# A hybrid decoder layer on one core: the u projection by channel, and a buffer for each row of x

## The chip, the core and the metric

The kernel runs on one core of a Trainium2 chip. TensorE (PE in the rows) multiplies, VectorE (DVE), ScalarE (ACT) and GpSimd (POOL) work on what it leaves, and SyncE (SP) issues nearly all transfers. The metric is the time of the device in microseconds for one execution of the program, taken as the median of several runs. Where a profile is read, it is that of one execution, and its time stands beside the median below.

## The reference

One layer of a decoder on 1024 prompt tokens and 8 sample tokens (1032 columns in all), 1024 channels. Only the first part matters here: a norm, one projection whose columns are split, and a state-space branch that eats the part called u.

```python
h = rms_norm(x, norm1_g)
proj = h @ w_in                        # 1024 x (512 q | 128 k | 128 v | 512 u | 2048 gates)
u = proj[..., o3:o4]                   # 512 channels = 32 groups of 16
...
attn_out = attend(q, k, v, sinks)      # window of 128
ug = u.reshape(B, T, 32, 16)
bu = einsum('gph,btgh->btgp', bb, ug)  # each group drives a complex state of 64
h  = associative_scan(...)             # over positions
y  = einsum('ghp,btgp->btgh', c, h) + d * u
z  = gelu(y); ssm_out = z * sigmoid(z @ w_glu + b_glu)
merged = sigmoid(g_a) * (attn_out @ w_a) + sigmoid(g_s) * (ssm_out @ w_s)
x = x + merged @ w_out;  x = x + swiglu_ffn(rms_norm(x)); y = rms_norm(x)
```

For the sample tokens the attention reads a window of 128 old keys and values (`state_k_win`, `state_v_win`), and the window moved on by one token is an output.

## The kernel before

All of it is f32. A product is done as three products of f32r halves (high x high, high x low, low x high), so each operand is split in two: `XH[k]`, `XL[k]` are the halves of row k of x (128 channels x 1032 tokens, k = 0 to 7), already multiplied by the norm's gain; `wuh`, `wul` are those of the u weights.

**The opening stage** (lines 178 to 274). For each row k, SP loads `xr` (three buffers of one tag, line 204), GpSimd issues the load of `wr` (line 211), ACT makes `XH` (L216), the squares `sq` (L224) and `wuh` (L214), DVE makes `XL` (L217), `wul` (L219) and adds the squares (L225). PE then multiplies by token: `umm(ps, k, slice(s, TP, 8))` holds every eighth column of x as the stationary operand (128 tokens of residue s modulo 8) and streams the 512 u channels, for s = 0 to 6 row by row as the rows come. After the last row, `rc` sums the squares over the channels (L232), `rstd` makes `rcol`, `uevac` takes each bank with the token's scale into `ut[b]`, then residue 7 and the eight sample tokens (`us`, with 8 stationary columns) follow, transposes turn the sample part, and `across` spreads `rcol` into `r1`, a row of scales by token.

**After it** come the projections k, v and four q (`load_w`, `mm3`, lines 467 to 512; three f32r matmuls of 344 columns for each of 8 rows and 3 chunks, 72 for a block of 128 channels). `load_w` passes weights through `wraw` (3 buffers), `wh` and `wl` (3 each): a load waits until the one three before it has been split. v is turned by transposes `vtp` (L490) that need `vt`, which DVE makes (L484). The attention's tables `msk`, `snk` and `snks` are loaded by SP; DVE makes `nsnk` from `snk` (L442). Then attention, its projection, the state-space stage (`group4`, eight times), and the feed-forward.

**In `group4`** four transposes (L805) turn `ut` into `ug`, ACT copies it to `UG` (L808), and both `sps` (L814) and `y` (L871) use `UG`.

**The order** on each engine is set by a scheduler at build time (`tc.block(schedule_with_timeline_sim=True)`), not by the text; each engine then runs its list in order and waits where an operand isn't there. The built program also makes each transfer of SP wait until the one some eight places ahead of it in the list has landed. Tags name places in memory: `Zl0` to `Zl3`, `Zh2`, `Zh3` and `s2` are of 128 x 1032 f32 and are used one after the other by what the text puts there.

## Time and profile before

| | |
|---|---|
| median of 3 runs | 1440.84 us (1439.7 to 1446.9) |
| the profiled execution | 1441.37 us, its span 1439.6 us |
| PE busy | 1362.9 us, 95% of the span |
| DVE, ACT, POOL busy | 874.7 (61%), 567.4 (39%), 460.4 us (32%) |
| PE clock by slices of 36 us | 0.9 or more of full speed, but 0.7 in the second, 0.8 in two later ones, 0.6 in the last |
| moved by DMA | 136.59 MB, 95 GB/s on the mean |

PE is the bound nearly everywhere: of the 40 slices of the page, PE shows 9 tenths or more in most. Two slices cover the opening stage. The rows below are read as follows: a timeline row gives when an instruction (or a run of like ones, x7) started, how long it was busy, its line, what it wrote from what, and in brackets how long its engine had been idle and what ended that.

### The profile page before, as it was taken

The numbers are of one execution on the slowest core, as the hardware profiler recorded it, in microseconds if no ns is written. First come the engines' busy times: TensorE is split into PE (matmuls) and PEld (weight loads), VectorE is DVE, ScalarE is ACT, GpSimd is POOL, SyncE is SP. The second block draws the span as 40 slices with busy tenths as digits, with TensorE's granted clock in tenths as the row PEclk, the third lists the DMA queues.
The fourth block names the chain that finished last, engine by engine and source line by source line (L and its number), as shares of the span: only waits on it lengthen the run. The fifth ranks groups of instructions, "written<-read, shape, count | busy, mean of one in ns | idle before, by whom it ended". The sixth has DMA issues, their size and how long they took to land. (4 is left out here: it accounts for less than half of the span.)

```text
span 1439.6 us, 25893 instructions
## 1 busy us (share of the span) xinstructions
PE 1362.9 (95%) x10031; PEld 1324.8 (92%) x10031; DVE 874.7 (61%) x1792; ACT 567.4 (39%) x1121; POOL 460.4 (32%) x411
## 2 busy tenths in 40 slices
PE   7699999998899999998899999999999999999995
PEld 6689999997788999997899999999999999999995
DVE  4575986259999744736485444444344674775864
ACT  3323656423344622434353333333333442433551
POOL 1113321156674000125144333333332132232352
PEclk9799999999989999999899999999999999999996
DMA  6102000121111201253534332332223882542413
GB/s 221 62 19 79 16 24 22 37 66 40 40 30 36 66 30 45 81 177 118 175 110 126 114 118 99 101 104 82 93 95 119 270 272 60 163 140 65 132 34 118
DMA packets 84731, 136.59 MB, mean 95 GB/s; under 512 B 15737, under 2 KB 27521, under 8 KB 84608
## 3 DMA queue, kind: packets, MB, share of 16 engines
q1 hardware_dynamic: 83248, 131.61, 28.8%
q0 software_dynamic: 640, 2.10, 0.5%
q8 instruction: 79, 1.29, 0.4%
q10 hardware_dynamic: 720, 1.23, 0.2%
q14 instruction: 44, 0.36, 0.1%
HBM read 103.59 MB, written 30.12 MB: 93 GB/s over the span
## 5 line engine op out<-in xcount | busy, mean ns | idle before, releaser
L126 PE MATMUL wo<-mh,wl_wo 128*128 128x258 f32 x256 | 74.0, 290 | 4.9 <-DVE wl_wo L114 4.9
L124 PE MATMUL wo<-mh,wh_wo 128*128 128x258 f32 x256 | 74.4, 290 | 2.5 <-ACT wh_wo L113 1.8
L125 PE MATMUL wo<-ml,wh_wo 128*128 128x258 f32 x256 | 73.7, 288 | 0.0
L126 PE MATMUL gs<-xh,wl_gs 128*128 128x344 f32 x192 | 61.7, 322 | 0.0
L124 PE MATMUL gs<-xh,wh_gs 128*128 128x344 f32 x192 | 61.6, 322 | 0.0
L125 PE MATMUL gs<-xl,wh_gs 128*128 128x344 f32 x192 | 61.5, 321 | 0.0
L1066 POOL TENSOR_TENSOR ws_d<-wr_1d,ws_d 128x512 f32<-128x512 f32 (+1 forms) x13 | 17.5, 1347 | 117.8 <-issue 74.5
L126 PEld LDWEIGHTS wo<-mh,wl_wo 128*128 128x128 f32 x256 | 49.9, 195 | 5.3 <-DVE wl_wo L114 5.3
L124 PEld LDWEIGHTS wo<-mh,wh_wo 128*128 128x128 f32 x256 | 50.1, 196 | 3.2 <-ACT wh_wo L113 3.2
L125 PEld LDWEIGHTS wo<-ml,wh_wo 128*128 128x128 f32 x256 | 49.9, 195 | 0.0
L126 PE MATMUL ga<-xh,wl_ga 128*128 128x344 f32 x144 | 47.5, 330 | 1.5 <-DVE wl_ga L114 1.5
L1066 POOL TENSOR_TENSOR ws_u<-wr_1u,ws_u 128x512 f32<-128x512 f32 x9 | 11.6, 1285 | 116.4 <-issue 116.4
L124 PE MATMUL ga<-xh,wh_ga 128*128 128x344 f32 x144 | 48.3, 335 | 0.0
L125 PE MATMUL ga<-xl,wh_ga 128*128 128x344 f32 x144 | 48.0, 333 | 0.0
L114 DVE TENSOR_TENSOR wl_wo<-wr_wo,wh_wo 128x512 fp32r<-128x512 f32 x32 | 23.0, 719 | 38.8 <-ACT wh_wo L113 38.7
L199 PE MATMUL u<-wuh,xh 128*128 128x512 f32 x64 | 24.8, 470 | 18.9 <-ACT wuh L214 17.1
L465 POOL TENSOR_TENSOR ml<-mg,mh 128x344 fp32r<-128x344 f32 x6 | 6.6, 1140 | 106.3 <-ACT mh L464 106.3
L199 PEld LDWEIGHTS u<-wuh,xh 128*128 128x128 f32 x64 | 19.2, 331 | 20.7 <-ACT wuh L214 17.4
L547 ACT ACTIVATE P<-P,st 128x256 f32<-128x256 f32 (+1 forms) x64 | 31.0, 486 | 17.5 <-DVE st L544 17.5
L113 ACT CAST wh_wo<-wr_wo 128x512 fp32r<-128x512 f32 x32 | 19.8, 620 | 41.4 <-PE wo L125 39.1
L124 PEld LDWEIGHTS gs<-xh,wh_gs 128*128 128x128 f32 x192 | 36.1, 188 | 0.0
L126 PEld LDWEIGHTS gs<-xh,wl_gs 128*128 128x128 f32 x192 | 36.0, 188 | 0.0
(2596 smaller groups left out, 5875.5 us busy)
## 6 DMA issues: line engine op xcount, KB each, us to landing
hr<-hid SPq DMA_DIRECT2D x77, 258.0 KB, 3.6
wr_wo<-in_wout SPq DMA_DIRECT2D x32, 256.0 KB, 2.9
wr_0g<-in_wfg SPq DMA_DIRECT2D x17, 256.0 KB, 3.1
wr_1g<-in_wfg SPq DMA_DIRECT2D x17, 256.0 KB, 2.9
wr_0u<-in_wfu SPq DMA_DIRECT2D x17, 256.0 KB, 2.7
wr_1u<-in_wfu SPq DMA_DIRECT2D x17, 256.0 KB, 2.6
xres<-in_xT SPq DMA_DIRECT2D x16, 258.0 KB, 3.8
x1d<-mg SPq DMA_DIRECT2D x16, 258.0 KB, 2.8
```

Source lines behind the costliest of these rows:

```text
L113: S.copy(wh[:, 0:w], raw[:, 0:w])
L114: (eng or V).tensor_tensor(wl[:, 0:w], raw[:, 0:w], f32(wh[:, 0:w]), op=ALU.subtract)
L124: TE.matmul(ps, wh, xh[:, cs], start=(k == 0), stop=False)
L125: TE.matmul(ps, wh, xl[:, cs], start=False, stop=False)
L126: TE.matmul(ps, wl, xh[:, cs], start=False, stop=(k == n - 1))
L199: TE.matmul(ps, XH[k][:, cs], wuh[:, k], start=(k == 0), stop=False)
L465: eng.tensor_tensor(lo, src, f32(hi), op=ALU.subtract)
L547: S.activation(Pt[:, i, 0:W], Pt[:, i, 0:W], AF.Exp, bias=nm_[:, i:i + 1], scale=0.125, accum_out=ds[:, i:i + 1])
L1066: P.tensor_tensor(t, x, y, op=op)
```

## The change

Four things are changed, and what depends on them.

1. **u by channel.** The u weights are now the stationary operand (128 channels m = 0 to 3) and x streams, in three chunks of 344 tokens: `umm(ps, m, k, c)`. The sample tokens ride in the last chunk. m = 0 and 1 take six banks and run row by row as the rows of x come; m = 2 and m = 3 run after the last row. The scale by token is now a product with `r1`, which lies along the columns, in `uput`; m = 1 is first taken unscaled by ACT and multiplied in place later.
2. **Reordered through DRAM.** `uput` writes `SG[m]` (channel, t, c) for token 8c + t, with the t steps 128 elements apart. `ushift` stores `SG[m]` to DRAM (`ud`) and loads it again in eight pieces of 16 partitions as `UGA[m]`, in the layout in which `group4` wants it. So the transposes `ug` and the copies `UG` are gone from `group4`, which takes a view of `UGA`.
3. **A buffer for each row of x.** The eight `xr` now lie in `Zl0` to `Zl3`, `Zh2`, `Zh3`, `s2` and one of their own; `ident` is loaded after the last row, and `wur` has five buffers where it had three.
4. **`Vs` whole.** The old values are loaded as 128 partitions where 127 were loaded; the host rolls the window, so that the last partition holds what is overwritten later.

```diff
@@ -174,14 +174,13 @@
     XM = [(XH[k], XL[k]) for k in range(KD)]
     r1 = main.tile([128, T], F32, tag="r", name="r1")
 
-
-    ut = [main.tile([128, 8, 8, 16], F32, tag=f"Zl{b}", name=f"ut{b}") for b in range(4)]
-
     ssmp = tc.tile_pool(name="ssmp", bufs=1, side="left")
     sp = ssmp.__enter__()
     usT = sp.tile([128, 4, NS], F32, tag="usT", name="usT")
 
 
+    ud = ctx.enter_context(tc.tile_pool(name="ud", bufs=1, space=bass.MemoryType.DRAM))
+    UGA = [None] * 4
     with tc.tile_pool(name="p1", bufs=1, side="left") as p1, \
             tc.tile_pool(name="p1r", bufs=1, side="right") as p1r:
         ssum = p1r.tile([128, T], F32, tag="ssum", name="ssum")
@@ -193,23 +192,26 @@
         wps = aux("warm", "pv")
         for i in range(12):
             TE.matmul(wps, warm[:, 0:128], warm, start=True, stop=True)
-        ups = [acc(f"u{s}") if s < 3 else aux(f"u{s}") for s in range(7)]
-
-        def umm(ps, k, cs):
-            TE.matmul(ps, XH[k][:, cs], wuh[:, k], start=(k == 0), stop=False)
-            TE.matmul(ps, XH[k][:, cs], wul[:, k], start=False, stop=False)
-            TE.matmul(ps, XL[k][:, cs], wuh[:, k], start=False, stop=(k == KD - 1))
-
+
+        def umm(ps, m, k, c):
+            wh, wl = wuh[:, k, 128 * m:128 * m + 128], wul[:, k, 128 * m:128 * m + 128]
+            TE.matmul(ps[:, :CH], wh, XH[k][:, chunk(c)], start=(k == 0), stop=False)
+            TE.matmul(ps[:, :CH], wh, XL[k][:, chunk(c)], start=False, stop=False)
+            TE.matmul(ps[:, :CH], wl, XH[k][:, chunk(c)], start=False, stop=(k == KD - 1))
+
+        UP = {(0, c): acc(f"u0{c}") for c in range(NCH)}
+        UP.update({(1, c): aux(f"u1{c}", "xxy"[c]) for c in range(NCH)})
         for k in range(KD):
-            xr = p1r.tile([128, T], F32, tag="xr", name=f"xr{k}", bufs=3)
-            wr = p1r.tile([128, 512], F32, tag="wur", name=f"wur{k}", bufs=3)
+            tag = ("Zl0", "Zl1", "Zl2", "Zl3", "Zh2", "Zh3", "s2", "xr")[k]
+            xr = (main if k < KD - 1 else p1r).tile([128, T], F32, tag=tag, name=f"xr{k}")
+            wr = p1r.tile([128, 512], F32, tag="wur", name=f"wur{k}", bufs=5)
             if k == 0:
                 for c in range(NCH):
                     (S if c == 1 else SY).dma_start(xr[:, chunk(c)], h["xT"][k][:, chunk(c)])
             else:
                 SY.dma_start(xr, h["xT"][k])
             P.dma_start(wr, h["wu"][k])
-            if k == 1:
+            if k == KD - 1:
                 SY.dma_start(ident, h["ident"])
             S.copy(wuh[:, k], wr)
             for cs in ([chunk(c) for c in range(NCH)] if k == 0 else [slice(0, T)]):
@@ -223,55 +225,79 @@
                 sq = p1r.tile([128, T], F32, tag="sq", name=f"sq{k}", bufs=1)
                 S.activation(sq, xr, AF.Square)
                 V.tensor_tensor(ssum, ssum, sq, op=ALU.add)
-            if k == KD - 1:
-
-                rc = aux("rc", "pv")
-                rcs = p1r.tile([128, 18], F32, tag="rcs", name="rcs")
-                V.memset(rcs, 1.0)
+            for m in range(2):
+                for c in range(NCH):
+                    umm(UP[m, c], m, k, c)
+
+
+        SG = [None] * 4
+        C8 = CH // 8
+
+        def uput(m, c, r):
+            if SG[m] is None:
+                SG[m] = main.tile([128, 8, 128], F32, tag=f"Zl{m}", name=f"sg{m}")
+            w = CH if c < NCH - 1 else CH - NS
+            dst = SG[m][:, :, c * C8:c * C8 + w // 8].rearrange("p t c -> p c t")
+            src = UP[m, c][:, 0:w].rearrange("p (c t) -> p c t", t=8)
+            if r:
+                V.tensor_tensor(dst, src, r1[:, c * CH:c * CH + w].rearrange("p (c t) -> p c t", t=8), op=ALU.mult)
+            else:
+                S.copy(dst, src)
+            if w < CH:
+                if r:
+                    V.tensor_tensor(usT[:, m], UP[m, c][:, w:CH], r1[:, TP:T], op=ALU.mult)
+                else:
+                    S.copy(usT[:, m], UP[m, c][:, w:CH])
+
+        def ushift(m):
+
+            t = ud.tile([128, 8, 128], F32, tag=f"ud{m}", name=f"ud{m}")
+            SY.dma_start(t, SG[m])
+            UGA[m] = main.tile([128, 8, 128], F32, tag=f"Zl{m}", name=f"ug{m}")
+            for i in range(8):
+                SY.dma_start(UGA[m][16 * (7 - i):16 * (8 - i)], t[:, i].rearrange("(g h) c -> h g c", h=16))
+
+        for c in range(NCH):
+            uput(1, c, False)
+
+        rc = aux("rc", "pv")
+        rcs = p1r.tile([128, 18], F32, tag="rcs", name="rcs")
+        V.memset(rcs, 1.0)
+        for c in range(NCH):
+            UP[2, c] = aux(f"u2{c}", "yxx"[c])
+            for k in range(KD):
+                umm(UP[2, c], 2, k, c)
+            if c == 0:
                 for s in range(8):
-                    TE.matmul(rc[:, 2 * s:2 * s + 2], ssum[:, s:TP:8], ones[:, 0:2], start=True, stop=True)
+                    colsum(rc, 2 * s, [ssum], 128 * s, 128)
                 colsum(rc, 16, [ssum], TP, NS)
                 V.tensor_copy(rcs[:, 0:16], rc[:, 0:16])
                 V.tensor_copy(rcs[:NS, 16:18], rc[:NS, 16:18])
                 rcol = rstd(p1r.tile([128, 4, 18], F32, tag="rcol", name="rcol"), rcs, 18)
-            for s in range(7):
-                umm(ups[s], k, slice(s, TP, 8))
-
-        def uevac(s, ps):
-            for b in range(4):
-                dst = ut[b][:, :, 7 - s, :]
-                src = ps[:, b * 128:(b + 1) * 128].rearrange("p (g h) -> p g h", h=16)
-                if s % 2 == 0:
-                    S.activation(dst, src, AF.Copy, scale=rcol[:, 2 * s:2 * s + 1])
-                else:
-                    V.tensor_scalar(dst, src, rcol[:, 2 * s:2 * s + 1], None, op0=ALU.mult)
-
-        for s in range(7):
-            uevac(s, ups[s])
-        u7 = aux("u7")
-        for k in range(KD):
-            umm(u7, k, slice(7, TP, 8))
-        uevac(7, u7)
-        usp = acc("us")
-        for k in range(KD):
-            umm(usp[:NS], k, slice(TP, T))
-        usm = p1r.tile([NS, 512], F32, tag="usm", name="usm")
-        V.tensor_scalar(usm, usp[:NS], rcol[:NS, 16:17], None, op0=ALU.mult)
-        ust = aux("ust", "pv")
-        for b in range(4):
-            TE.transpose(ust[:, b * NS:(b + 1) * NS], usm[:, b * 128:(b + 1) * 128], ident[:NS, :NS])
-        V.tensor_copy(usT, ust[:, 0:4 * NS].rearrange("p (b t) -> p b t", b=4))
-
-        r1v = r1[:, 0:TP].rearrange("p (c t) -> p t c", t=8)
         for q in range(3):
-            rp = aux(f"r1p{q}")
+            rp = aux(f"r1p{q}", ("pv", "y", "pv")[q])
             if q < 2:
                 for i in range(4):
                     across(rp, 128 * i, rcol[:, 8 * q + 2 * i:8 * q + 2 * i + 1], 128)
-                S.copy(r1v[:, 4 * q:4 * q + 4], rp.rearrange("p (t c) -> p t c", t=4))
+                S.copy(r1[:, 512 * q:512 * q + 512], rp)
             else:
                 across(rp, 0, rcol[:, 16:17], NS)
                 S.copy(r1[:, TP:T], rp[:, 0:NS])
+        for c in range(NCH):
+            uput(0, c, True)
+        ushift(0)
+        V.tensor_tensor(SG[1], SG[1], r1[:, 0:TP].rearrange("p (c t) -> p t c", t=8), op=ALU.mult)
+        V.tensor_tensor(usT[:, 1], usT[:, 1], r1[:, TP:T], op=ALU.mult)
+        ushift(1)
+        for c in range(NCH):
+            uput(2, c, True)
+        ushift(2)
+        for c in range(NCH):
+            UP[3, c] = acc(f"u3{c}")
+            for k in range(KD):
+                umm(UP[3, c], 3, k, c)
+            uput(3, c, True)
+        ushift(3)
 
         def pt(name, shape=(128, 48), pool=None):
             return (pool or sp).tile(list(shape), F32, tag=name, name=name)
@@ -442,7 +468,7 @@
     V.tensor_scalar(nsnk, snk, -1.0, None, op0=ALU.mult)
     SY.dma_start(snks, h["sinks_s"])
     SY.dma_start(Ks, h["ks"])
-    SY.dma_start(Vs[0:127], h["vs"])
+    SY.dma_start(Vs, h["vs"])
     for c in range(NCH):
         V.tensor_tensor(Cr[:, chunk(c)], Cr[:, chunk(c)], r1[:, chunk(c)], op=ALU.mult)
         V.tensor_tensor(Sr[:, chunk(c)], Sr[:, chunk(c)], r1[:, chunk(c)], op=ALU.mult)
@@ -799,13 +825,7 @@
         for s in range(8):
             SY.dma_start(M[16 * s:16 * s + 16, :, 16 * (7 - s):128], kt[:, :, 0:16 * (s + 1)])
 
-
-        tp = aux(f"ug{hb}", "x")
-        for i in range(4):
-            TE.transpose(tp[:, i * 128:(i + 1) * 128],
-                         ut[b][:, 4 * half + i].rearrange("p a b -> p (a b)"), ident)
-        UG = t4("UG", (128, 4, 128), 2)
-        S.copy(UG.rearrange("p a b -> p (a b)"), tp)
+        UG = UGA[b][:, 4 * half:4 * half + 4]
 
 
         next(fill, None)
...
-    a["vs"] = vs[:, 1:].transpose(1, 0, 2)
+    a["vs"] = np.roll(vs, -1, axis=1).transpose(1, 0, 2)
```

What the scheduler makes of it is shown at three places.

SP at the start of the program, before: `xr3` to `xr6` are the fourth to seventh rows of x, `Cr` and `Sr` the rotary tables, `Ks` and `Vs` the old keys and values, `wr_k`, `wr_v` the weights of k and v.

```order
L437 DMA Cr_761<-in_rope_c 128x1032
L438 DMA Sr_762<-in_rope_s 128x1032
L444 DMA Ks_763<-in_ks 128x1024
L210 DMA xr3_224<-in_xT 128x1032
L445 DMA Vs_764<-in_vs 127x1024
L107 DMA wr_k_0_784<-in_wst 128x512
L107 DMA wr_k_512_790<-in_wst 128x512
L107 DMA wr_v_0_904<-in_wst 128x512
L210 DMA xr4_256<-in_xT 128x1032
L210 DMA xr5_288<-in_xT 128x1032
L210 DMA xr6_320<-in_xT 128x1032
L107 DMA wr_v_512_910<-in_wst 128x512
```

And after (the first six rows of x stand ahead of these, with no other load between them):

```order
L212 DMA xr6_298<-in_xT 128x1032
L212 DMA xr7_327<-in_xT 128x1032
L215 DMA ident_66<-in_ident 128x128
L315 DMA sgn_618<-in_sgn 128x1
L320 DMA prm_624<-in_prm 128x144
L463 DMA Cr_860<-in_rope_c 128x1032
L464 DMA Sr_861<-in_rope_s 128x1032
L107 DMA wr_k_0_883<-in_wst 128x512
L107 DMA wr_k_512_889<-in_wst 128x512
L107 DMA wr_v_0_1003<-in_wst 128x512
L470 DMA Ks_862<-in_ks 128x1024
L471 DMA Vs_863<-in_vs 128x1024
```

All eight rows of x are now issued ahead of every other load of SP; before, three of them stood behind `Vs` and three weight loads, and the last behind three more.

SP later, after: `ud1`, `ud2`, `ud3` are the stores of u to DRAM and `ug0` to `ug3` the loads that bring it back (eight each), `snk` the sinks from which DVE makes `nsnk`.

```order
L258 DMA ug1_493<-ud1_491 16x8x128 x8
L258 DMA ug2_509<-ud2_507 16x8x128 x8
L255 DMA ud3_598<-sg3_543 128x1024
L258 DMA ug3_600<-ud3_598 16x8x128 x8
L107 DMA wr_q1_0_1233<-in_wst 128x512
L107 DMA wr_q1_512_1239<-in_wst 128x512
L501 DMA out_kwp<-ro_k2_995 128x128
L503 DMA out_kws<-Ks_862 128x1024
L465 DMA msk_865<-in_mask 128x256
L466 DMA snk_866<-in_sinks 128x8
```

The same stretch before has no transfer of u in it:

```order
L107 DMA wr_q0_0_1016<-in_wst 128x512
L107 DMA wr_q0_512_1022<-in_wst 128x512
L210 DMA xr7_352<-in_xT 128x1032
L439 DMA msk_766<-in_mask 128x256
L440 DMA snk_767<-in_sinks 128x8
L443 DMA snks_768<-in_sinks_s 64x1
L107 DMA wr_q1_0_1134<-in_wst 128x512
L107 DMA wr_q1_512_1140<-in_wst 128x512
L475 DMA out_kwp<-ro_k2_896 128x128
L477 DMA out_kws<-Ks_763 128x1024
```

Thirty-six transfers of u now stand between the first weights of q0 and those of q1, and `msk`, `snk` and `snks`, which stood ahead of q1's weights, now stand behind them and behind two outputs.

DVE around `nsnk`, before (`kl` is the low half of k, `vt` is v with its scale):

```order
L465 TENSOR_TENSOR kl_758<-ro_k0_826,kh_757 128x344
L460 TENSOR_TENSOR ro_k1_861<-ro_k1_861,rs_k1_858 128x344
L442 TENSOR_SCALAR nsnk_773<-snk_767 128x8
L465 TENSOR_TENSOR kl_758<-ro_k1_861,kh_757 128x344
L456 STREAM_SHUFFLE rs_k2_893<-rr_k2_891 128x344
L459 TENSOR_TENSOR ro_k2_896<-k2_866,Cr_761 128x344
L460 TENSOR_TENSOR ro_k2_896<-ro_k2_896,rs_k2_893 128x344
L476 COPY Ks_763<-ro_k2_896 128x8
L465 TENSOR_TENSOR kl_758<-ro_k2_896,kh_757 128x344
L484 TENSOR_TENSOR vt_916<-v0_917,r1_83 128x344
L484 TENSOR_TENSOR vt_916<-v1_943,r1_83 128x344
L484 TENSOR_TENSOR vt_916<-v2_969,r1_83 128x344
```

and after:

```order
L510 TENSOR_TENSOR vt_1015<-v0_1016,r1_83 128x344
L491 TENSOR_TENSOR kl_857<-ro_k0_925,kh_856 128x344
L491 TENSOR_TENSOR kl_857<-ro_k1_960,kh_856 128x344
L491 TENSOR_TENSOR kl_857<-ro_k2_995,kh_856 128x344
L468 TENSOR_SCALAR nsnk_872<-snk_866 128x8
L510 TENSOR_TENSOR vt_1015<-v1_1042,r1_83 128x344
L510 TENSOR_TENSOR vt_1015<-v2_1068,r1_83 128x344
L519 TENSOR_TENSOR vl_859<-vtp0_1095,vh_858 128x512
L524 COPY vsm_1111<-vts_1109 8x128
```

`nsnk`, which waits for `snk`, stood ahead of the last `ro_k` and of all three `vt`; now it stands between the first `vt` and the other two, and PE's transposes `vtp` stand right behind the last product of v on PE in both.

## Rows read from the trace of the kernel before

**Rows 1.** Who waited for whom: total us, times, longest; 0 to 130 us.

```profile
PE u L199 <- ACT wuh L214: 17.1, 1, 17.1
```

**Rows 2.** Stretches: busy us (count) of PE, PEld, DVE, ACT, POOL; clock, DMA share, GB/s.

```profile
10.00:20.00 10.00, 10.00 (x38) 9.45 (x38) 9.13 (x25) 7.41 (x9) 1.61 (x3) 0.89 0.79 302
38.00:40.00 2.00, 0.00 (x0) 0.00 (x0) 0.00 (x0) 0.00 (x0) 0.00 (x0) 0.50 0.07 27
30.00:48.00 18.00, 0.87 (x3) 0.55 (x2) 2.07 (x4) 5.11 (x7) 3.71 (x3) 0.57 0.41 137
70.00:77.00 7.00, 7.00 (x20) 5.64 (x21) 5.64 (x32) 3.43 (x13) 0.00 (x0) 0.51 0.00 0
296.00:460.00 164.00, 145.15 (x937) 135.04 (x936) 146.03 (x287) 61.99 (x130) 112.11 (x120) 0.95 0.15 41
```

**Rows 3.** Timeline (start us, us, engine, line, operation) of SP's issues, 0 to 140.

```profile
9.95 0.56 SPq L445 DMA_DIRECT2D Vs<-in_vs  x1
10.80 15.81 SPq L107 DMA_DIRECT2D wr_k<-in_wst  x2
28.19 6.37 SPq L210 DMA_DIRECT2D xr<-in_xT  x3
```

**Rows 4.** Timeline of PE in the opening stage and in the k projection.

```profile
7.85 2.87 PE L199 MATMUL u<-wuh,xh 128*128 128x512 f32 x7 [1.79 <-ACT xh L216]
...
47.42 3.38 PE L199 MATMUL u<-wuh,xh 128*128 128x512 f32 x7 [17.13 <-ACT wuh L214]
...
67.16 3.74 PE L232 MATMUL rc<-ones,ssum 128*128 128x2 f32 x16
...
90.89 0.40 PE L124 MATMUL k<-xh,wh_k 128*128 128x344 f32 x1
...
94.47 0.32 PE L125 MATMUL k<-xl,wh_k 128*128 128x344 f32 x1
...
96.05 0.32 PE L126 MATMUL k<-xh,wl_k 128*128 128x344 f32 x1
```

**Rows 5.** Weight loads grouped by line (busy us, mean ns), 60 to 90 and 90 to 112.

```profile
L199 PEld LDWEIGHTS u<-wuh,xh 128*128 128x128 f32 x22 | 7.3, 331 | 0.3
...
L124 PEld LDWEIGHTS k<-xh,wh_k 128*128 128x128 f32 x24 | 4.5, 188 | 0.0
```

**Rows 6.** Timeline of ACT and DVE over one row of x.

```profile
9.51 1.16 ACT L216 ACTIVATE xh<-xr,vec 128x1032 fp32r<-128x1032 f32 x1 [0.76 <-DMA xr<-in_xT]
...
10.70 1.29 DVE L217 SCALAR_TENSOR_TENSOR xl<-xr,vec,xh 128x1032 fp32r<-128x1032 f32 x1 [2.29 <-ACT xh L216]
...
12.04 1.16 ACT L216 ACTIVATE xh<-xr,vec 128x1032 fp32r<-128x1032 f32 x1
...
13.66 0.18 DVE L310 TENSOR_SCALAR t<-prm 128x48 f32<-128x48 f32 x1
```

**Rows 7.** PSUM copies, ns min/median/max, and one DVE product from PSUM (timeline).

```profile
L271 ACT COPY r<-r1p x2: 1159/1194/1228, 90.7 to 91.7; 128x512 f32<-128x512 f32 x2
L808 ACT COPY UG<-ug x8: 566/567/584, 323.4 to 453.8; 128x512 f32<-128x512 f32 x8
...
105.50 0.50 DVE L459 TENSOR_TENSOR ro_k<-k,Cr 128x344 f32<-128x344 f32 x1
```

**Rows 8.** Small pieces on SP and their landing: timeline; issues with KB, us to landing.

```profile
100.76 0.43 SPq L440 DMA_DIRECT2D snk<-in_sinks  x1
...
324.16 5.20 SPq L800 DMA_DIRECT2D M<-kt  x8
...
bc<-in_bc SPq DMA_DIRECT2D x4, 256.0 KB, 3.1
```

**Rows 9.** Timeline of DVE at `nsnk` and at the last chunk of v.

```profile
104.31 0.17 DVE L442 TENSOR_SCALAR nsnk<-snk 128x8 f32<-128x8 f32 x1 [0.68 <-DMA snk<-in_sinks]
...
114.32 0.52 DVE L484 TENSOR_TENSOR vt<-v,r 128x344 f32<-128x344 f32 x1 [3.25 <-PE v L126]
```

**Rows 10.** Timeline of PE: the four transposes of one `group4`.

```profile
320.58 0.60 PE L805 MATMUL ug<-ident,ut 128*128 128x128 f32 x4
```

## The prediction

> **What bounds the kernel now.** I read the stretches first, then the waits, then the timeline of SP and PE in the first 115 us. PE is the bound almost everywhere, so a change pays for the PE time that it removes, and for holes in PE, and for nothing else unless it opens a hole. There is one large hole in the stage that the change touches: between 30 and 48 us PE was busy for 0.87 us of 18, at a clock of 0.57 on the mean, and DMA, too, at 0.41 of its share [rows 2]. The wait behind it is the longest of PE in the stage, 17.1 us for `wuh` [rows 1]; ACT makes `wuh` behind `xh`, which waits for a row of x. SP shows why the row was late: `Vs` was issued at 9.95, the two weight loads behind it held SP for 15.81 us, and the next three rows of x went out only at 28.19 [rows 3]. In the middle of the hole DMA moved 27 GB/s at a share of 0.07, which is one engine of 16 [rows 2]: something was passing through a single engine while all else had to wait. `Vs`, of 127 partitions, is the only load here of that odd shape. PE began u at 7.85, went on at 47.42 after 17.13 us of nothing, and reached the first product of k at 90.89 [rows 4]. So the stage up to k takes 90.9 us.
>
> **What the change does to the stage.** I build the time of k's first product anew.
>
> *Rows of x.* All eight are issued ahead of all else, into buffers of their own. Rows and u weights are 6.3 MB; at the 302 GB/s of 10 to 20 us [rows 2] the last lands at about 23, earlier if the rate is higher. The engines that split them are slower than that: ACT needs 12.04 - 9.51 = 2.53 us a row, DVE 13.66 - 10.70 = 2.96 [rows 6]. DVE is the pacer. From its 10.70, seven rows are 20.7 us, and some 2.4 us of small operations (16 of about 0.15; one alone is 0.18) lie between; without the last addition of squares, which PE doesn't need, `wul` of the last row is there at about 31.5.
>
> *PE, first part.* A product of 344 columns takes 1.58/10 = 0.158 us (94.47 to 96.05, ten of them) [rows 4]. The row-by-row part has 2 x 3 x 3 = 18 a row, 2.84 us, so PE follows DVE and ends the last row at 34.5. Nothing of the 17.1 us hole is left, since no row waits for a buffer or for `Vs`.
>
> *PE, second part.* The first chunk of m = 2, 24 x 0.158 = 3.8; the column sums `rc`, 3.74 and 0.2 for the sample tokens, 3.9 [rows 4]; two more chunks, 7.6; the low clock behind `rc` (0.51 of full speed in 70 to 77 [rows 2]) stays, and I carry 2.6 for it: 6 us of work at half rate lose 3, and the sums may be shorter. The `across` products are 18 of about 0.15 (0.60 for four of that width [rows 10]), 2.7. Before m = 3 can start, ACT copies `r1` and DVE scales a bank; most of that lies beside the last `across`, 0.3 shows. m = 3 is 72 x 0.158 = 11.4. The sum is 34.5 + 3.8 + 3.9 + 7.6 + 2.6 + 2.7 + 0.3 + 11.4 = 66.8, against 90.9: **24.1 us less**. Of this the hole is 17; the rest is that 288 products of 344 columns take 45.5 us where token products were bound by weight loads of 331 ns (strided columns of x) against 188 for k's [rows 5], and that residue 7 and the sample tokens no longer stand alone.
>
> *SP, behind it.* This is the cost. Four stores and 32 loads stand in SP ahead of q1's weights, `msk` and `snk`; `nsnk` waits for `snk` on DVE, and behind it stand `vt` of chunks 1 and 2, for which PE waits with `vtp` before it can start q. I measure from t, the moment that `r1` is ready, 12.3 us ahead of k's first product; v's last product ends 144 x 0.158 = 22.8 after that, at t + 35.1. Up to the last scaled chunk of m = 2 DVE has six such chunks, two products for the rotary tables, the product in place of 1024 columns and some small ones. If a chunk costs what a product from PSUM costs now, 0.50 and some 0.43 from one to the next [rows 7], that is 2.6 + 0.9 + 1.3 + 0.8 = 5.6 us. No row shows DVE writing single words 512 bytes apart. The nearest is ACT's copy of `r1`, words 32 bytes apart: 1194 ns against 566 for as many contiguous [rows 7]. With twice the price for the strided ones it is 9.5. SP's small pieces follow at 5.20/8 = 0.65 us each [rows 8]: 24 of them to t + 21.6; the fourth store, landing like a 256 KB load in small pieces, 3.1 [rows 8], to t + 25.1; eight loads to t + 30.3; five issues ahead of `snk` and its own, 2.0; landing, from 100.76 to 104.31, 3.5 [rows 8, 9]; `nsnk` and `vt`, 0.17 and 0.52 [rows 9]: t + 36.5. PE would wait 1.4 us, with the doubled price 5.3. I take 3.3, between the two, as the strided row is of another engine, and 1.2 for the clock that falls in such a gap: behind 1.79 us of idle seven products took 2.87 us, behind 17.13 us 3.38 [rows 4], where at full speed they take some 1.9: **4.5 us more**, from 0 to 8. Before, `snk` kept DVE for 0.68 us and PE for nothing [rows 9].
>
> The Trainium skill bears on that unknown: "SBUF — State Buffer", Door 1: The DMA port swizzle, says that SBUF is read and written in lines of 16 bytes and that each step to a new line costs extra. By it the doubled price is right and the wait is 5.3 rather than 3.3. The strided weight loads and the ACT copy agree with it; for DVE no run here shows it.
>
> *State-space stage.* Per `group4` four transposes of 0.60 us together [rows 10] and a copy of 0.57 on ACT [rows 7] go, eight times: 4.8 us of PE. From 296 to 460 PE was busy for 145.15 of 164 us and DVE for 146.03 [rows 2], so DVE is as much the bound there, and its work is the same. I take half, **2.4 us less**, between nothing and 4.8. The scheduler puts DVE's and PE's work there in another order, too, which may cost or save some 3 us; I take none.
>
> *At no cost:* the reloads `ug` land by about t + 33, near 90 us, and are first used after 300; four megabytes of traffic lie where DMA is nearly idle. The whole `Vs` is issued after x, and `wr_k` ahead of it.
>
> **How the numbers follow.** -24.1 + 4.5 - 2.4 = -22.0. The profiled execution took 1441.4 us (span 1439.6), 0.5 above the median of three; from it, 1419. PE is full from v to 296, so what is won in the first 90 us isn't lost again there.
>
> **The rivals.**
>
> *The start is paced by DMA.* Eight rows of x in flight with the weights share one path, and ACT has `wr_k` and `wr_v` ahead of its last two `wuh`, so the first 8.2 MB count. At 302 GB/s they land at 29.5, 1 to 2 us late at that place; a quarter slower at 38, and u's rows end 7 us later: 1426. For it: ACT sat idle for x before 9.51 already [rows 6]. Against it: the 302 holds waits for buffers as well. Chance 0.12.
>
> *The clock stays low in the row-by-row part.* PE has gaps of under a microsecond in each row, and 1.79 us of idle were followed by slow products [rows 4]. At half rate a row is 5.7 us, more than its feeders need, so the gaps then close and it can't last; half the rows are +8: 1427. Chance 0.07.
>
> *No wait at `vtp`,* with SP's pieces cheaper: 1414.5; within the forecast's case.
>
> *Slower: the reorder holds SP too long.* Every 0.1 us more for a small piece makes 3.2 us more of wait, once it is the last to end; all of the 22 us is gone at 0.65 + 22/32 = 1.34 us a piece, and at 1.6 it is 1449. For it: no row shows a load from DRAM into 16 partitions in 512-byte runs. Against it: `bc`, of such runs and four times as large, landed in 3.1 us [rows 8], and with eight in flight that allows 0.4 us each. Chance 0.03.
>
> *It doesn't do what it says:* x is late for another reason than buffers and `Vs`, and half the hole comes back, at another place: 1430. Against it: SP's list has nothing ahead of x. Chance 0.04.
>
> **Chances and range.** The forecast's case (1411 to 1427, by the wait of 0 to 8, the state-space part from -5.5 to +1, and 2 us on the row pace) has 0.74; the first two rivals lie at its upper edge. For 8 times in 10 the range is 1409 to 1430. A change of 0.5%, 7.2 us, is about what a measurement of this kernel can tell from none. Faster by more than that, below 1433.6: 0.93; within: 0.04; slower: 0.03.
>
> **What would show it.** Right: no idle of PE above 2 us between 8 and 65 us, and its clock at full speed between rows; the first product of k at 65 to 69; the rows of x landed by 23; `wul` of row 7 near 31; SP's `ug` loads at 0.65 us each; a wait of DVE for `snk` of some us and one of PE at `vtp`; a state-space stage shorter by 0 to 5 us. Wrong: the first product of k after 72 (then look at whether ACT waits for `xr` or `wr_k`, or the clock is at half), or at 60 (then DVE's pace was misread); PE waiting at q1 or in the first `attend`, with SP still issuing `ug` past 110 us.

## The result, and the profile after

The changed kernel took 1425.38 us in the median of four runs (1423.21 to 1426.52) against 1440.27 us of the kernel before on the same chip: a ratio of 0.9885, 95% interval 0.9852 to 0.9917. A second series gave 1423.18 against 1443.65, 0.9867 (0.9846 to 0.9889). So it is faster by 15 to 20 us; 22 were forecast, 1419 in a range of 1409 to 1430. Of all executions below one took far longer than the others of its kernel, 3232.19 us of `s1_ug` against 1412.34 to 1417.19; it is in that kernel's median and not in its ratio.

The profiled execution took 1426.52 us (span 1424.7). I cut both traces at the same products: the first of k, the first of q, the first `smt` (state-space stage begins), the last `zp` (it ends), the last of `ps`, the last of `r3c`. Between these marks stand the same stages. The columns are those of [rows 2]. First the kernel before:

```profile
0.00:90.90 90.90, 70.66 (x267) 60.28 (x267) 51.04 (x211) 30.66 (x49) 8.93 (x16) 0.83 0.33 112
90.90:114.58 23.68, 23.68 (x154) 23.42 (x153) 15.05 (x48) 6.97 (x13) 6.88 (x6) 1.00 0.16 54
114.58:308.40 193.82, 193.26 (x1315) 182.64 (x1314) 120.71 (x413) 99.24 (x285) 50.40 (x64) 1.00 0.13 38
308.40:485.40 177.00, 158.15 (x1027) 148.01 (x1026) 159.63 (x315) 73.55 (x152) 105.11 (x112) 0.95 0.15 41
485.40:599.70 114.30, 114.29 (x727) 114.01 (x726) 65.64 (x128) 40.46 (x81) 6.64 (x6) 1.00 0.15 44
599.70:1425.20 825.50, 799.75 (x6543) 793.65 (x6541) 457.95 (x670) 315.69 (x542) 279.95 (x206) 0.98 0.39 125
```

and the changed one:

```profile
0.00:62.00 62.00, 56.42 (x336) 52.28 (x337) 52.03 (x167) 29.03 (x39) 11.04 (x16) 0.97 0.55 197
62.00:86.25 24.25, 23.33 (x152) 23.07 (x150) 20.91 (x87) 4.97 (x10) 7.50 (x7) 1.00 0.47 147
86.25:280.40 194.15, 193.50 (x1316) 182.66 (x1314) 120.72 (x412) 99.06 (x284) 49.27 (x64) 1.00 0.12 38
280.40:455.40 175.00, 149.91 (x935) 140.19 (x936) 159.65 (x313) 67.57 (x140) 100.13 (x112) 0.90 0.15 39
455.40:578.50 123.10, 123.10 (x785) 123.10 (x783) 67.81 (x132) 42.96 (x85) 6.65 (x6) 1.00 0.14 44
578.50:1410.70 832.20, 802.67 (x6541) 795.71 (x6541) 455.80 (x670) 315.44 (x542) 278.70 (x206) 0.98 0.39 124
```

Stage by stage that is -28.9, +0.6, +0.3, -2.0, +8.8 and +6.7 us. The opening gave more than the whole gain. The state-space stage is 2.0 us shorter, but the records show 92 products fewer of PE in it (935 against 1027; 32 are the transposes `ug` that are gone, the others nearly all products of the gates, 596 in place of 653), and the stretch behind it, where PE never waits, has 58 more: taken together the two cost 6.8. At the last `ps` the kernel leads by 21.2 us; the rest of the loss lies in a part that the change doesn't touch.

The waits of PE that answer to [rows 1] (0 to 130 us: total, times, longest):

```profile
PE u L198 <- ACT wuh L216: 3.3, 3, 2.3
PE vtp L516 <- DVE vt L510: 0.9, 1, 0.9
PE u L200 <- DVE wul L221: 0.7, 1, 0.7
```

The wait of 17.1 us is gone. SP's list (timeline, as [rows 3]) shows all rows of x ahead of everything, and the reorder behind:

```profile
2.13 4.36 SPq L212 DMA_DIRECT2D xr<-in_xT  x7
...
28.60 0.33 SPq L471 DMA_DIRECT2D Vs<-in_vs  x1
...
53.53 3.79 SPq L255 DMA_DIRECT2D ud<-sg  x3
57.41 12.67 SPq L258 DMA_DIRECT2D ug<-ud  x24
70.18 0.37 SPq L255 DMA_DIRECT2D ud<-sg  x1
73.13 3.62 SPq L258 DMA_DIRECT2D ug<-ud  x8
...
81.76 0.45 SPq L466 DMA_DIRECT2D snk<-in_sinks  x1
```

### The profile page after: what moved, and what is told of

It reads as the page before. It is cut to its first block, busy times and chain, and to the rows that moved or that the text cites. A ratio compares the mean times of both kernels' runs of the same rounds, so it can differ in the third digit from the quotient of the medians.

```text
span 1424.7 us, 25963 instructions
## 1 busy us (share of the span) xinstructions
PE 1352.1 (95%) x10067; PEld 1319.9 (93%) x10067; DVE 881.6 (62%) x1788; ACT 559.8 (39%) x1101; POOL 455.8 (32%) x411
## 5 line engine op out<-in xcount | busy, mean ns | idle before, releaser
L125 PEld LDWEIGHTS gs<-xl,wh_gs 128*128 128x128 f32 x192 | 36.6, 191 | 0.0
L198 PE MATMUL u<-xh,wuh 128*128 128x344 f32 x96 | 31.9, 338 | 3.5 <-ACT wuh L216 3.3
```

Of the source, the lines that this page charges most:

```text
L125: TE.matmul(ps, wh, xl[:, cs], start=False, stop=False)
L198: TE.matmul(ps[:, :CH], wh, XH[k][:, chunk(c)], start=(k == 0), stop=False)
```

## The experiments

Two questions: which part of the change shortened the opening, and what took some 7 us back around the state-space stage. Each kernel was timed against the kernel before on the same chip.

**Vs whole, alone** (`b1_vs`).

```diff
-    SY.dma_start(Vs[0:127], h["vs"])
+    SY.dma_start(Vs, h["vs"])
...
-    a["vs"] = vs[:, 1:].transpose(1, 0, 2)
+    a["vs"] = np.roll(vs, -1, axis=1).transpose(1, 0, 2)
```

> The kernel before, with one thing of the change: Vs loaded whole, as 128 partitions, in place of 127; x keeps its three rotating buffers and u is still projected by token. Theory 1 (the one transfer of Vs that moves on a single engine, behind which the later rows of x stand, made most of the hole in the opening): the first product of k comes 12 to 17 us earlier than at 90.9 us, and the kernel takes 1424 to 1428 us. Rival (the row buffers are what counts, since row 3 of x must wait for a buffer in any case): the first product of k comes at most 4 us earlier, 1436 to 1440 us.

Measured: k's first product at 69.8 us, 21.1 earlier; 1422.05 us, ratio 0.9877 (0.9857 to 0.9897). Theory 1 holds in kind, but both numbers lie beyond its ranges: one line of the change alone is as fast as all of it. Two stretches of this kernel, the first that of the first of [rows 2]:

```profile
10.00:20.00 10.00, 10.00 (x40) 9.73 (x40) 9.39 (x26) 7.15 (x9) 1.61 (x3) 0.95 1.00 392
20.00:30.00 10.00, 10.00 (x43) 10.00 (x42) 9.86 (x23) 6.65 (x9) 4.84 (x3) 1.00 0.76 290
```

All 16 engines move data where one moved 27 GB/s, and PE has no hole. A second look at the same kernel (`b3_xv`):

> The kernel before with Vs whole, a second look at b1_vs: theory 1 gives the first product of k at 69 to 71 us again, the stage 176 to 178 us and the stretch behind it 114 us; any other value would say that these stretches scatter between executions.

It gave 69.9, 176.6 and 114.4 us, and 1423.77 in its one execution: these stretches repeat to a few tenths.

**A buffer for each row of x, alone** (`b2_x`).

```diff
-            xr = p1r.tile([128, T], F32, tag="xr", name=f"xr{k}", bufs=3)
+            if k < 3:
+                xr = p1r.tile([128, T], F32, tag="xr", name=f"xr{k}", bufs=3)
+            else:
+                xr = main.tile([128, T], F32, tag=("Zh2", "Zh3", "s2", "Zh0", "Zh1")[k - 3], name=f"xr{k}")
```

> The kernel before, with a buffer for each row of x (rows 3 to 7 in tiles that are written later anyway) so that all seven whole-row loads are issued first; Vs still 127 partitions, u still by token. Theory 1 (rows of x that arrive late were the whole loss of the opening, and the projection by channel adds nothing to that): the first product of k at 68 to 74 us, 1418 to 1424 us, no slower than the changed kernel's 1425.4. Rival (the projection by channel is what shortened the opening): the first product of k not before 80 us, 1429 to 1437 us.

Measured: 69.1 us; 1421.48 us, 0.9874 (0.9854 to 0.9894). With x in front, the slow `Vs` harms nobody. So either repair is enough, since by token PE needs some 5 us for a row (21 products; 43 took 10.00 us above) and is itself the bound: it waited 1.8 us in all for u.

**By channel with three buffers** (`a2_x3`).

```diff
-            tag = ("Zl0", "Zl1", "Zl2", "Zl3", "Zh2", "Zh3", "s2", "xr")[k]
-            xr = (main if k < KD - 1 else p1r).tile([128, T], F32, tag=tag, name=f"xr{k}")
+            xr = p1r.tile([128, T], F32, tag="xr", name=f"xr{k}", bufs=3)
```

> The changed kernel with x in three rotating buffers again; u by channel and Vs whole stay. Theory 1: Ks and Vs (0.5 MB each) go ahead of the rows of x from 3 on, the first product of k comes 3 to 6 us later than at 62.0, 1428 to 1431 us. Rival (once Vs is whole the order of the loads no longer matters): 1424 to 1427 us.

Measured: 69.1 us, 7.1 later than with the buffers; 1427.74 us, 0.9921 (0.9899 to 0.9944). The direction is theory 1's, the delay somewhat more and the time just under its range. Now PE waits for x:

```profile
PE u L198 <- ACT xh L217: 3.9, 2, 2.4
PE u L199 <- DVE xl L218: 3.6, 1, 3.6
```

The four openings: by token with a whole `Vs` 69.8, by token with buffers 69.1, by channel with a whole `Vs` 69.1, by channel with both 62.0. The channel form without buffers gains 0.7 us over the token form, and the token form is 0.7 apart with either repair; channel form and buffers together gain 7. (By token with both repairs wasn't run; PE is the bound there already.)

**The transposes put back** (`s1_ug`). From here on it is the stage that is asked about.

```diff
-        UG = UGA[b][:, 4 * half:4 * half + 4]
+        tp = aux(f"ug{hb}", "x")
+        for i in range(4):
+            TE.transpose(tp[:, i * 128:(i + 1) * 128], UGA[b][:, 4 * half + i], ident)
+        UG = t4("UG", (128, 4, 128), 2)
+        S.copy(UG.rearrange("p a b -> p (a b)"), tp)
```

> The changed kernel with the 32 transposes of ug and their 8 copies on ScalarE put back into the state-space stage (they now transpose what is already reordered, so the values of the outputs that depend on u differ). Its PE order has 653 products of the gates between the first smt and the last zp, as the kernel before; the changed kernel has 596, and 57 products (9.2 us at the full clock) stand behind the stage. Theory 2 (the order that the scheduler chose without the transposes took back 7 to 9 us of the gain): the stretch from the last zp to the last product of ps is 114 us again in place of 123, the stage not longer than 178 us, and the kernel takes 1416 to 1420 us though it does more. Rival (the stage is bound by VectorE, and gate products placed in it lengthen it by as much as they save behind it): the stage is 182 us or longer, 1424 to 1428 us.

Measured: 1416.91 us, 0.9825 (0.9806 to 0.9844), some 7 us faster than the changed kernel with more to do. PE's order in the stage and the stretch behind it is that of the kernel before, product for product, and the two take as long as there:

```profile
281.60:459.50 177.90, 159.00 (x1026) 148.58 (x1026) 159.28 (x317) 73.71 (x153) 105.45 (x112) 0.95 0.15 41
459.50:573.70 114.20, 114.18 (x727) 113.91 (x725) 65.66 (x128) 40.33 (x81) 6.65 (x6) 1.00 0.15 44
```

**The same work in a worse order** (`s2_ugd`): as `s1_ug`, but `UG` remains the view of `UGA`, and the copy goes to a tile that nobody reads.

```diff
         UG = UGA[b][:, 4 * half:4 * half + 4]
+        ...
+        UG2 = t4("UG", (128, 4, 128), 2)
+        S.copy(UG2.rearrange("p a b -> p (a b)"), tp)
```

> As s1_ug, with the same 32 transposes and 8 copies put back, but their results are read by nobody: the state-space stage reads the reordered u directly, as the changed kernel does. The scheduler now puts only 571 products of the gates between the first smt and the last zp, where s1_ug has 653. Theory 2 (the number of gate products that the order places in the stage sets the time): 82 products more stand behind the stage than in s1_ug, 13 us at the full clock, some of it given back by a stage that is 1 to 5 us shorter; from the last zp to the last product of ps 126 to 128 us, the kernel 1424 to 1430 us, 8 to 13 above s1_ug. Rival (the added instructions themselves made s1_ug fast, as by holding PE's clock up): 1416 to 1420 us, as s1_ug.

Measured: 1426.00 us, 0.9885 (0.9861 to 0.9909), stretch 126.9 us. As theory 2 said: the same instructions, some 9 us apart.

```profile
279.70:454.80 175.10, 147.58 (x944) 137.74 (x944) 161.41 (x310) 69.47 (x146) 98.60 (x112) 0.91 0.14 37
454.80:581.70 126.90, 126.90 (x809) 126.90 (x807) 69.92 (x135) 44.58 (x88) 6.64 (x6) 1.00 0.15 46
```

What differs is the order, and that `sps` and `y` no longer read the copy; in `s1_ug` PE waited 0.5 us for it. That a wait less makes a kernel slower isn't to be expected, but no run here separates the two.

**One more step of the gates per group** (`s3_fill3`).

```diff
                 S.copy(dst[64 * gg:64 * gg + 64], spv[64 * q:64 * q + 64, :, gg])
+        next(fill, None)
```

> The changed kernel with one more step of the gates written into each group of the state-space stage, behind the copies of sps. No instruction is added or left out; the scheduler's order changes, with 629 gate products in the stage in place of 596. Theory 2: 33 products fewer behind the stage, 5.3 us, less 0 to 2 by which the stage gets longer: 1420 to 1422 us, last zp to last ps 117 to 118 us. Rival (the stage is bound by VectorE, so what is moved into it lengthens it by as much): 1425 us.

Measured: the stretch behind is 117.8 us as said, but the stage 179.4, 4.4 longer; 1420.93 us, 0.9855 (0.9830 to 0.9880). The time lies in theory 2's range, but its interval overlaps that of the changed kernel in the same series (0.9846 to 0.9889), so it can't decide. The stretches can: together they are 297.2 against 298.1, as by the rival's mechanism. What was moved in lengthened the stage by nearly as much; the count of placed products alone is not the cause.

**Gate steps on GpSimd** (`n1_pool`).

```diff
-            w = load_w(h["wst"][6 + m], 1024, f"ga{m}", tags=WT.get(m))
+            w = load_w(h["wst"][6 + m], 1024, f"ga{m}", P, tags=WT.get(m))
...
-                V.tensor_tensor(MG[m][:, chunk(c)], MG[m][:, chunk(c)], t, op=ALU.mult)
+                P.tensor_tensor(MG[m][:, chunk(c)], MG[m][:, chunk(c)], t, op=ALU.mult)
```

> The changed kernel with two steps of the gates in the state-space stage moved from VectorE to GpSimd: the low half of the ga weights and the product of mg with the gate (17 of 0.84 us and 7 of 0.9 us in the changed kernel's stage, some 20 us of VectorE's 160). The scheduler then places 682 gate products in the stage. Theory 2 with VectorE as the bound of the stage: the stage is 165 to 175 us, last zp to last ps 109 to 112 us, the kernel 1405 to 1416 us. Rival (GpSimd, with 100 of 175 us busy and slower at such products, becomes the bound): the stage is 178 us or longer, 1418 to 1426 us.

Measured: stage 193.3 us; 1430.63 us, 0.9919 (0.9899 to 0.9938), slower than the changed kernel and than either forecast. The rival's direction, but not by its mechanism: GpSimd was busy 121 of 193 us, and DVE didn't get lighter. The stage:

```profile
282.80:476.10 193.30, 165.50 (x1022) 154.44 (x1023) 161.63 (x290) 69.79 (x145) 121.26 (x137) 0.91 0.14 39
```

DVE had 23 instructions fewer than in the changed kernel's stage (290 against 313) and was busy for 161.6 us against 159.7. One product of 128 x 256 in both (mean ns behind the bar), first the changed kernel, then this one:

```profile
L861 DVE TENSOR_TENSOR W<-RE,TC 128x256 f32<-128x256 f32 x8 | 5.7, 716 | 0.8 <-ACT RE L839 0.4 <-POOL dd L822 0.4
L873 DVE TENSOR_TENSOR W<-RE,TC 128x256 f32<-128x256 f32 x8 | 3.2, 398 | 0.0
```

```profile
L861 DVE TENSOR_TENSOR W<-RE,TC 128x256 f32<-128x256 f32 x8 | 10.9, 1358 | 2.4 <-POOL TC L855 1.9 <-POOL dd L822 0.4
L873 DVE TENSOR_TENSOR W<-RE,TC 128x256 f32<-128x256 f32 x8 | 3.2, 400 | 0.0
```

**The copy of IN on VectorE** (`i_inv`). In the changed kernel the longest wait of PE in the stage was `kp` for `IN` (total us, times, longest), and here is one of the two on PE's timeline:

```profile
PE kp L818 <- ACT IN L814: 8.9, 2, 6.1
...
317.80 0.61 PE L812 MATMUL inp<-ident,INT 128*128 128x128 f32 x4
...
324.90 1.44 PE L818 MATMUL kp<-OUT,bst 128*16 128x128 f32 x6 [2.71 <-ACT IN L814]
```

ACT's timeline shows why: the copy of what PE had ready at 318.4 stands behind `ga` and `gt`, which wait for DVE.

```profile
322.31 0.63 ACT L896 ACTIVATE ga<-ga 128x512 f32<-128x512 f32 x1 [7.81 <-DVE ga L895]
323.70 0.58 ACT L619 ACTIVATE gt<-gt,vec 128x344 f32<-128x344 f32 x1 [0.76 <-DVE gt L617]
324.19 0.57 ACT L814 COPY IN<-inp 128x512 f32<-128x512 f32 x1
```

```diff
-        S.copy(IN.rearrange("p a b -> p (a b)"), tp)
+        V.tensor_copy(IN.rearrange("p a b -> p (a b)"), tp)
```

> The changed kernel with the copy of IN (8 of 128 x 512 from PSUM) on VectorE in place of ScalarE. In the changed kernel PE waits 8.9 us for that copy, which stands on ScalarE behind a sigmoid gt that waits for VectorE. Theory 4 (what the changed order lost in the state-space stage is PE idling behind ScalarE's queue): the wait of kp for IN goes to under 2 us, stage plus stretch to the last product of ps from 298.0 to 290 to 294 us, the kernel 1416 to 1420 us. Rival (VectorE, busy 160 of 175 us, bounds the stage, and 8 copies of some 0.65 us more on it lengthen it by 5): stage plus stretch 297 to 301 us, 1422 to 1427 us.

Measured: that wait is gone, 1420.58 us, 0.9862 (0.9838 to 0.9886); stage and stretch 295.8; both lie between the two forecasts. Another wait has come, again for DVE, whose busy time rose to 167.4:

```profile
PE smp L771 <- DVE x L769: 13.3, 3, 6.1
```

**And two buffers for INT** (`j_inv_int2`): `t4("INT", (128, 4, 8, 16), 2)` on top.

> As i_inv, and INT has two buffers, so that GpSimd can build the next group's INT while PE still reads this one's; the order then has 658 gate products in the state-space stage (the changed kernel 596, the kernel before 653). Theory 4: stage plus stretch to the last product of ps 288 to 293 us, 1414 to 1419 us. Rival (VectorE bounds the stage): 297 to 301 us, 1422 to 1427 us.

Measured: stage 184.9, stretch 113.5, together 298.4: the rival's. The median, 1420.48 (0.9857, 0.9833 to 0.9881), lies in neither range and is no lower than that of `i_inv`, with more products placed.

**The changed kernel again** (`a0_again`), for the part behind `ps`.

> The changed kernel once more, for a second profiled execution. From the first product of ps on, its PE order is that of the kernel before, product for product; in the first profile this part took 832.2 us (last product of ps to last product of r3c) against 825.5 before. Theory 3 (a difference of this size there is scatter between executions of one program): this profile has 824 to 830 us there, with the opening (first product of k at 62.0) and the state-space stage (175.0) as in the first within 0.5 us; the median is 1423 to 1427 us. Rival (something that the change leaves behind slows that part): 831 to 834 us again.

Measured: 1423.18 us; opening 62.3, stage 174.9, stretch 123.1, all as before, and the rest 824.3 in place of 832.2:

```profile
578.80:1403.10 824.30, 797.15 (x6541) 790.93 (x6541) 457.88 (x670) 315.77 (x542) 278.77 (x206) 0.99 0.39 125
```

So the +6.7 there was scatter between executions. In the twelve profiles of kernels whose PE order in that part is the same it went from 822.0 to 832.2 us.

**The identity as a copy** (`c1_id`): as `s1_ug`, but PE passes the reordered u through unturned.

```diff
-        UG = UGA[b][:, 4 * half:4 * half + 4]
+        tp = aux(f"ug{hb}", "x")
+        for i in range(4):
+            TE.matmul(tp[:, i * 128:(i + 1) * 128], ident, UGA[b][:, 4 * half + i], start=True, stop=True)
+        UG = t4("UG", (128, 4, 128), 2)
+        S.copy(UG.rearrange("p a b -> p (a b)"), tp)
```

> The changed kernel, with PE copying the reordered u through PSUM in each group of the state-space stage (32 products with the identity as weights, 8 copies on ScalarE), so that all values are right; the work added is useless in itself. The scheduler's order is near that of s1_ug, with 642 gate products in the stage. Theory 2 (the order that goes with these products is worth more than they cost): stage plus stretch to the last product of ps 291 to 294 us as in s1_ug (292.1) and the kernel before (291.3), where the changed kernel has 298.0; 1415 to 1419 us. Rival (the low time of s1_ug came from its values or from chance): 297 to 300 us, 1422 to 1426 us.

Measured: 1417.62 us, 0.9828 (0.9810 to 0.9846), stage 177.5 and stretch 115.8, together 293.3. Of the kernels whose u is right it is the fastest here, some 6 us below the changed one, for a copy that computes nothing.

Side by side, from one profile each; the idle time is the stage less PE's busy time in it:

| kernel | gate products in the stage | stage, us | PE idle, us | clock | to the last `ps`, us | sum, us |
|---|---|---|---|---|---|---|
| before | 653 | 177.0 | 18.8 | 0.95 | 114.3 | 291.3 |
| changed | 596 | 175.0 | 25.1 | 0.90 | 123.1 | 298.1 |
| `b1_vs` | 653 | 176.8 | 20.9 | 0.96 | 114.3 | 291.1 |
| `s1_ug` | 653 | 177.9 | 18.9 | 0.95 | 114.2 | 292.1 |
| `c1_id` | 642 | 177.5 | 18.4 | 0.95 | 115.8 | 293.3 |
| `i_inv` | 642 | 180.0 | 26.0 | 0.93 | 115.8 | 295.8 |
| `s3_fill3` | 629 | 179.4 | 28.6 | 0.93 | 117.8 | 297.2 |
| `j_inv_int2` | 658 | 184.9 | 25.4 | 0.93 | 113.5 | 298.4 |
| `a2_x3` | 596 | 175.3 | 30.1 | 0.93 | 123.1 | 298.4 |
| `s2_ugd` | 571 | 175.1 | 27.5 | 0.91 | 126.9 | 302.0 |
| `n1_pool` | 682 | 193.3 | 27.8 | 0.91 | 112.6 | 305.9 |

The stretch behind goes with the count alone: from 571 to 658 products placed it falls from 126.9 to 113.5 us, 0.154 us a product. So what an order is worth is how little its stage grows by the products that it takes in. Against the changed kernel, the order of the kernel before and of `s1_ug` takes in 57 more for 2.0 and 2.9 us, `c1_id` 46 for 2.5; `s3_fill3` takes 33 for 4.4, `i_inv` 46 for 5.0, `j_inv_int2` 62 for 9.9.

PE's idle time and clock go with that (18 to 21 us at 0.95 or 0.96 for the kernel before, `b1_vs`, `s1_ug` and `c1_id`, 25 to 30 at a lower clock for the others), but they don't set the stage's length by themselves. `a2_x3` has the changed kernel's order in stage and stretch on PE, DVE, ACT and GpSimd, instruction for instruction, a higher clock and 5 us more of idle time, and a stage as long, 175.3 against 175.0:

```profile
286.60:461.90 175.30, 145.22 (x936) 135.40 (x937) 159.91 (x313) 67.13 (x140) 100.13 (x112) 0.93 0.14 39
```

So the faster PE only waited longer. That the order separates these four from the others is shown by `s1_ug` against `s2_ugd`, as far as these two differ in nothing else that counts; which property of an order does it is not. Taking one wait away (`i_inv`) brought another. That stays open.

## Why the prediction came out near

The time was inside the range, and at the last `ps` the lead of 21.2 us is nearly the 22.0 forecast. But that is luck: three errors, -4.8 in the opening, -3.9 at `vtp` and +9.2 at the state-space stage, nearly cancel.

*The opening: right in mechanism, 4.8 us too small.* -24.1 was forecast, -28.9 measured. No row of x waits for a buffer or for `Vs` any more, as said, and the last one, issued at 6.0 us, landed 13.8 us later (forecast: by 23). DVE had no slack, as said, busy for 14.70 of the 14.70 us from 20.0 to 34.7, but PE didn't simply follow it: PE was busy for 13.96 of them and waited for DVE once, 0.74 us. Up to the column sums the time is right, 38.3 forecast and 38.53 measured, though the last `wul` ended at 34.67 and not at 31.5 (the prediction's own terms, 10.70 + 20.7 + 2.4 less some 1.2 for the last addition, give 32.7). The delay cost nothing because PE takes the products with `wul` last: 24 of its 168 were left when it came, where the prediction had 42. DVE's small operations are part of the delay: one of 128 x 48 took 1.31 us while GpSimd made the low half of k's weights, and 0.19 later, while GpSimd was idle.

```profile
25.48 3.18 POOL L114 TENSOR_TENSOR wl_k<-wr_k,wh_k 128x512 fp32r<-128x512 f32 x1 [5.82 <-ACT wh_k L113]
...
27.39 1.31 DVE L337 TENSOR_SCALAR t<-t 128x48 f32<-128x48 f32 x1
...
39.17 0.19 DVE L337 TENSOR_SCALAR t<-t 128x48 f32<-128x48 f32 x1
```

The terms behind it were too large:

```profile
38.53 1.97 PE L153 MATMUL rc<-ones,ssum 128*128 128x2 f32 x18
...
48.08 2.26 PE L157 MATMUL r1p<-ident,rcol 128*128 128x128 f32 x18
...
50.58 0.42 PE L198 MATMUL u<-xh,wuh 128*128 128x344 f32 x1 [0.25 <-DVE sg L243]
```

`rc` cost 1.97 and not 3.9: its old weights were columns of `ssum` eight apart, loaded in 334 ns each, the new ones lie together, 180 ns (first the kernel before, then the changed one).

```profile
L232 PEld LDWEIGHTS rc<-ones,ssum 128*128 128x128 f32 x16 | 3.9, 334 | 0.0
L153 PEld LDWEIGHTS rc<-ones,ssum 128*128 128x128 f32 (+1 forms) x18 | 2.0, 180 | 0.0
```

The prediction had this effect for u [rows 5] and didn't apply it to `rc`. The low clock behind `rc`, 2.6, didn't come: the clock is 1.00 from 20 to 62. `across` cost 2.3 and not 2.7. These three are 5.0 us, less 0.2 by which `rc` began later.

*The credit.* "Of this the hole is 17" put the repair of x's loads too low and gave the channel form 7 of its own. By `b1_vs` the repair alone is 21.1, as the slow products behind the hole go with it; what the channel form adds is 7, and only with the buffers.

*The wait at `vtp`: 4.5 forecast, 0.6 measured.* The chain of the lower bound ended where it was said to: `vt` at t + 36.5, which from 49.7 is 86.2; it ended at 86.3.

```profile
85.30 0.17 DVE L468 TENSOR_SCALAR nsnk<-snk 128x8 f32<-128x8 f32 x1 [2.41 <-DMA snk<-in_sinks]
85.38 0.93 DVE L510 TENSOR_TENSOR vt<-v,r 128x344 f32<-128x344 f32 x2
```

That sum held the single price of a strided chunk, and that it comes out is luck, as its parts erred against each other: pieces took 0.53 and 0.45 us and not 0.65; a chunk took 0.78, where the ends were 0.50 and 1.0; and `snk` was issued 5.0 us behind the last piece, where it was given 2.0 with its own issue. PE waited 0.92 us, and the clock stayed at 1.00, so neither the middle value of 3.3 nor the 1.2 for the clock was needed. The lower bound, 1.4, was the nearest.

*The state-space stage: -2.4 forecast, +6.8 measured.* This is the step that failed. The stage itself is 2.0 shorter, and DVE's busy time in it is the same to 0.1 us, as said. But "may cost or save some 3 us; I take none" put at nothing what became the largest error: in the order that the scheduler chose without the transposes 57 products of the gates fewer stand in the stage, and the stretch behind, which the prediction didn't count, grew by 8.8. PE has some 13.8 us less to do (4.8 of transposes, 9.0 of gates) in a stage that is only 2.0 shorter: 6.2 became idle time, the rest went with a clock of 0.90 in place of 0.95. The order of the changed kernel was there to be read before any run: 596 products in place of 653, and 57 x 0.16 = 9 us is what the stretch grew by.

*The rivals.* None came true at its price. Loads did hold the first rows a little: from 10 to 20 us DMA was at its full share with 402 GB/s, and ACT waited 3.2 us in all for u's weights and rows of x. But the rival had 302 GB/s, and PE's waits for `wuh` came to 3.3 us. The clock was low in the first rows alone (0.88 from 8 to 20 us, 1.00 from 20 on), and no reorder held SP too long.

## What to carry over

Before a stage is rewritten, look at what stands in front of its loads: one transfer of an odd shape cost 21 us here, and either giving it its full shape or issuing the urgent rows ahead of it repaired that, with no new algorithm and as fast as the whole change. Where a scheduler orders the engines, removing instructions from a stage bound by another engine isn't a gain until the new order has been read: count the independent products that it leaves inside the stage, and compare the sum of the stage and the stretch behind it, not the stage alone. And a gain that needs two edits together (here channel form and buffers) shows in neither edit alone, so measure them apart and together.

## What the runs showed of the hardware

*The one-engine transfer.* The share of 0.07 and the 27 GB/s of [rows 2] were `Vs` of 127 partitions: with 128 the stretch from 10 to 20 us moved 392 GB/s at a share of 1.00, with nothing else changed. The Trainium skill, "DMA: Bandwidth & Descriptors", section "Why a DMA increments its semaphore by 16 and not by 1", says that a transfer is spread over the largest number of engines up to 16 that divides its outer size, one for 127. The trace agrees.

*GpSimd slows VectorE.* In `n1_pool` the product of 128 x 256 at L861 went from 716 to 1358 ns, while the same form at L873, where GpSimd was idle but once, stayed at 398 and 400. Of the eight at L861 six took 0.97 to 4.07 us, each beside GpSimd for most of it, and two 0.41 and 0.43; in the changed kernel two took 1.59 and 1.68, beside GpSimd too, and six 0.40 to 0.42. Not all of GpSimd's work does it: some of the fast ones lay beside it as well. The Trainium skill, "Perfetto Trace Analysis", section "Optimizing Scalar/DVE Operations", warns that the two share a port and that moving work between them might not help; here the moved work bought nothing: 161.6 us busy against 159.7. That it is the port, no run here shows.

*Strided writes.* Writing words 512 bytes apart, DVE took 0.78 us for 344 columns from PSUM, and ACT 0.81:

```profile
L243 DVE TENSOR_TENSOR sg<-u,r x9: 746/781/817, 49.8 to 63.2; 128x344 f32<-128x344 f32 x6, 128x336 f32<-128x336 f32 x3
L245 ACT COPY sg<-u x3: 798/810/859, 37.2 to 38.4; 128x344 f32<-128x344 f32 x2, 128x336 f32<-128x336 f32 x1
```

DVE's contiguous product took 0.50 [rows 7], so the factor is 1.6; ACT's contiguous copy of as many columns took 0.44 in this kernel, a factor of 1.8. The extra cost for new lines that the prediction quoted from the Trainium skill ("SBUF — State Buffer", Door 1: The DMA port swizzle) is there, but it isn't a doubling; the page gives no factor, the prediction took two from ACT's copy.
